# A hybrid decoder trunk on one core: scratch buffers placed by the plan, sums kept in the tiles of x, and a planner that lets two engines wait

## The chip, the cores and the metric

The kernel runs on one core of a Trainium2 chip. The core has a matrix engine (TensorE, PE; its weight loads are the rows PEld), a vector engine (VectorE, DVE), a scalar engine (ScalarE, ACT), GpSimd (POOL), and a queue that issues nearly all transfers (SyncE, SP). Each engine runs its own list of instructions strictly in order, and waits on semaphores for the others. The metric is device time of one execution in microseconds (us). The kernel before took 2038.9 us, the median of three runs (2038.4 to 2039.33).

## The reference

Two layers on an x of 1024 tokens by 1024 channels in float32:

```
for l in range(2):
    h = rmsnorm(x, attn_norm[l]);  proj = h @ w_in[l]
    c_q, c_kv, k_r, g_b, g_c, u_conv, u_pool, q_sw, k_sw, v_sw = split(proj)
    y_a = latent attention(c_q, c_kv, k_r)      # 4 heads, causal, rotary part
    y_b = g_b * conv3(g_c * u_conv)             # short gated convolution
    y_c = pool(u_pool)                          # causal means over 2/4/8/16
    y_d = sliding-window attention(q_sw, k_sw, v_sw)
    mixed = [y / rms(y) for y in (y_a, y_b, y_c, y_d)] * mix_norm[l]
    x = x + mixed @ w_o[l]
    gate, up = split(rmsnorm(x, ffn_norm[l]) @ w_gate_up[l])
    x = x + (silu(gate) * up) @ w_down[l]
return rmsnorm(x, final_norm)
```

The result must be accurate to float32, so each operand of a product is split into a high and a low part (ScalarE casts the high one, VectorE subtracts for the low one), and a product is three matmuls: high by high, high by low, low by high.

## The kernel before

Everything is kept transposed: 128 channels on the partitions, tokens along the row, in two halves of 512. Large tiles live in 47 pairs of slots (`Slots`), each pair 128 x 1024 in four-byte words; small scratch tiles of 128 x 512 come from `tmp`, which has three rings: 2 tiles "te", 3 "tn", 3 "tp". Sums of matmuls go to the eight PSUM banks.

Each layer has a *mixer stage* (about 50 to 430 us and 1050 to 1440 us of the profiled span): the projections, the four mixers, their norms and the output projection. It has many short steps in which TensorE, ScalarE and VectorE hand work to each other. Then come the FFN (to about 800 and 1800 us) and the down-projection. Both use a scheme with seven products in place of eight for 2 x 2 blocks, over the two halves of tokens and pairs of channel blocks, for which sums and differences of the operands are needed: `combine(j)` makes those of x for channel blocks 2j and 2j+1 (its inputs are named a0, b0, a1, b1, the two blocks in the two token halves; its results N1, N2, T3, T4), and `GateUp.sums` those of the weights, on GpSimd.

The lines that the text speaks of: `mm3` (L344) issues nearly all matmuls; `split` (L364 and L367 without a gain, L369 and L370 with one) splits operands; `weights` (L238, L239; L231 where the low part was prepared) splits a weight tile; `mul_to` (L445) multiplies two tiles; `SumSq.rnorm` (L424 to L439) makes the reciprocal of a root mean square; `scores` (L1064 to L1066 the products of queries and keys, L1069 to L1102 the softmax); `mix_values` (L1118, L1130); `combine` (L1229 to L1240, with `minus`, L1219); in the FFN, `GateUp.start`, `n2` (L1358 copies a PSUM bank out), `n1` (L1366), `snap` (L1408), `neg_mul` (L1534), `silu` (L1540 on ScalarE, L1542 the multiplication on GpSimd).

What sets the order of the work is a planner, `Order`, that runs while the program is built. It has a cost for each instruction, walks the program by list scheduling (of what is ready on an engine, the one with the lowest rank starts; ranks come from a pass from the end backwards), tries some thirty random changes near the places where its model has TensorE wait, and imposes the best order on every engine. From its planned end times it also picks the PSUM bank of each PSUM tile (`banks`) and the slot pair of each large tile (`ends`). `scheduled_kernel` does this for two settings (`SLOW`, the costs of VectorE and ScalarE as they are or 3% up) and takes the plan with the best mean over trials with random delays. The rule by which an engine takes its next operation is in `run`:

```
due(e, t)                          # what is ready by t goes into now[e]
k = heapq.heappop(now[e])[1]       # the lowest rank of these starts
```

## Time and profile before

| | |
|---|---|
| time, median of 3 runs | 2038.9 us (2038.4 to 2039.33) |
| profiled execution, first to last instruction (span) | 2037.3 us |
| granted TensorE clock, mean | 0.998 |
| PE busy | 2022.8 us, 99% of the span |
| VectorE busy | 1541.0 us, 76% |
| ScalarE busy | 1020.8 us, 50% |
| GpSimd busy | 565.8 us, 28% |
| HBM traffic | 170 GB/s over the span |

The profile has no other time of that execution than its span; the median of the runs is 1.6 us above it.

How to read its rows: in a row of the timeline stand the start, the duration, the engine, the line, the operation, output and inputs, partitions by elements, the count of instructions merged into the row, and in brackets the idle time before it and what ended it. A matmul's record is longer than the step from one matmul to the next, since matmuls overlap. In a row of a table of stretches stand the stretch, its length, the busy time (with the number of instructions) of PE, PEld, DVE, ACT and POOL, the granted clock as a share, the share of DMA busy and GB/s.

### The profile page before, as it was taken

Reading aid. Unit: us, or ns where it says so; the run is one execution under the profiler, and the core shown is the slowest. Engines: PE = TensorE matmul, PEld = TensorE weight load, DVE = VectorE, ACT = ScalarE, POOL = GpSimd, SP = SyncE. Lnnn points to the kernel's source line nnn. Section 1 sums busy time; section 2 is a strip of 40 time slices with the busy share of each in tenths; the row PEclk is TensorE's granted clock in tenths of the full one; section 3 lists DMA queues with packets and bytes.
Section 4 is the critical chain, followed back from the end, with each engine's and each line's share of the span. In section 5 each row is a group of like instructions: output and inputs, shape, how many; then the busy total and the mean of one; then the engine's idle time right before and its main releaser. Section 6 shows DMA issues by size and latency. Waiting matters only on the chain.

```text
span 2037.3 us, 26734 instructions
## 1 busy us (share of the span) xinstructions
PE 2022.8 (99%) x9418; PEld 1678.6 (82%) x9418; DVE 1541.0 (76%) x2442; ACT 1020.8 (50%) x1778; POOL 565.8 (28%) x428
## 2 busy tenths in 40 slices
PE   9999999999999999999999999999999999999998
PEld 7887888878888888888888878888888888888887
DVE  8779979997667768767646898889976766875555
ACT  7447657753333335555533676677433333354343
POOL 0100000047776782000001000000677777710000
PEclk9999999999999999999999999999999999999999
DMA  6431232434555546998835233242455555487552
GB/s 210 104 64 47 72 102 82 149 124 170 183 182 185 180 169 246 364 349 314 288 113 122 63 93 122 92 144 94 147 192 172 193 175 172 155 308 254 178 186 85
DMA packets 154087, 338.56 MB, mean 166 GB/s; under 512 B 14944, under 2 KB 62048, under 8 KB 153952
## 3 DMA queue, kind: packets, MB, share of 16 engines
q1 hardware_dynamic: 149472, 325.31, 46.3%
q0 software_dynamic: 4480, 11.54, 3.2%
q8 instruction: 74, 1.21, 0.3%
q14 instruction: 61, 0.50, 0.1%
HBM read 241.36 MB, written 105.91 MB: 170 GB/s over the span
## 4 chain that ended last, share of the span: by engine, by line
PE 95%; DVE 2%; DMA 1%; issue 1%; ACT 1%; POOL 0%; SPq 0%; DVEq 0%; POOLq 0%; ACTq 0%
PE ps_mm L344 37%; PE ps_s L344 28%; PE ps_t L344 12%; PE ps_pv L344 8%; PE ps_pv L1130 2%; PE ps_t L1118 1%; PE ps_s L1064 1%; PE ps_s L1066 1%; PE ps_s L1065 1%; PE ps_s L678 1%; PE ps_s L936 1%; PE ps_pv L739 1%; PE ps_t L727 1%; DVE u L367 1%; PE ps_t L424 0%
## 5 line engine op out<-in xcount | busy, mean ns | idle before, releaser
L344 PE MATMUL ps_mm<-u,u 128*128 128x512 f32 (+1 forms) x3378 | 832.4, 390 | 2.2 <-DVE tn L436 0.6
L344 PEld LDWEIGHTS ps_mm<-u,u 128*128 128x128 f32 x3378 | 617.4, 188 | 124.9 <-issue 3.1
L367 DVE TENSOR_TENSOR u<-u,u 128x1024 fp32r<-128x1024 f32 (+3 forms) x429 | 497.0, 1181 | 193.2 <-ACT u L364 131.4
L344 PE MATMUL ps_s<-u,u 128*128 128x512 f32 x2670 | 635.1, 390 | 0.7 <-ACT u L1358 0.5
L364 ACT CAST u<-u 128x1024 fp32r<-128x1024 f32 (+3 forms) x429 | 370.6, 882 | 438.6 <-PE ps_mm L344 62.4
L344 PEld LDWEIGHTS ps_s<-u,u 128*128 128x128 f32 x2670 | 501.5, 188 | 106.2 <-ACT u L1358 1.4
L344 PE MATMUL ps_t<-u,u 128*128 128x512 f32 (+1 forms) x1124 | 256.2, 378 | 0.1
L344 PEld LDWEIGHTS ps_t<-u,u 128*128 128x128 f32 x1124 | 202.7, 188 | 41.2 <-DVE u L1534 2.5
L1542 POOL TENSOR_TENSOR tp<-tp,u 128x512 f32<-128x512 f32 x80 | 126.9, 1586 | 347.8 <-ACT tp L1540 211.3
L344 PE MATMUL ps_pv<-u,u 128*128 128x512 f32 x744 | 177.3, 390 | 0.0
L344 PEld LDWEIGHTS ps_pv<-u,u 128*128 128x128 f32 x744 | 139.7, 188 | 28.9
L318 POOL DMA_DIRECT2D gd<-in_w_gu x24 | 21.2, 885 | 416.3 <-PE ps_t L344 280.9
L1127 POOL MEMSET u<- 128x128 f32 x32 | 6.3, 222 | 426.7 <-PE ps_pv L1130 117.6
L1540 ACT ACTIVATE tp<-tp 128x512 f32<-128x512 f32 x80 | 50.6, 632 | 131.5 <-DVE tp L445 131.4
L364 ACT CAST u<-ps_t 128x512 fp32r<-128x512 f32 (+3 forms) x132 | 64.6, 503 | 55.4 <-PE ps_t L1118 29.1
L367 DVE TENSOR_TENSOR u<-ps_t,u 128x512 fp32r<-128x512 f32 (+3 forms) x132 | 74.8, 581 | 13.9 <-ACT u L364 13.1
L1620 POOL TENSOR_TENSOR u<-u 128x352 f32<-128x352 f32 x64 | 79.3, 1240 | 9.8 <-DMA u<-in_w_dn 9.2
L369 ACT ACTIVATE u<-u,par 128x512 fp32r<-128x512 f32 x99 | 69.5, 717 | 23.3 <-DVE u L445 9.4
L1620 POOL TENSOR_TENSOR u<-u,u 128x352 f32<-128x352 f32 x64 | 76.7, 1199 | 2.6
L370 DVE SCALAR_TENSOR_TENSOR u<-u,par,u 128x512 fp32r<-128x512 f32 x99 | 72.9, 749 | 5.3 <-ACT u L369 5.2
L445 DVE TENSOR_TENSOR tp<-tp,u 128x512 f32<-128x512 f32 x76 | 73.9, 973 | 2.0
L1330 POOL TENSOR_TENSOR u<-u 128x512 f32<-128x512 f32 x38 | 67.4, 1773 | 27.3 <-DVE u L367 27.3
(209 smaller groups left out, 2316.6 us busy)
## 6 DMA issues: line engine op xcount, KB each, us to landing
u<-in_w_gu SPq DMA_DIRECT2D x84, 512.0 KB, 4.0
ad<-u SPq DMA_DIRECT2D x154, 256.0 KB, 2.3
u<-ad SPq DMA_DIRECT2D x70, 512.0 KB, 5.6
u<-in_w_dn SPq DMA_DIRECT2D x64, 352.0 KB, 3.5
qd<-u SPq DMA_DIRECT2D x64, 352.0 KB, 3.1
u<-in_w_in SPq DMA_DIRECT2D x43, 512.0 KB, 5.8
u<-qd SPq DMA_DIRECT2D x32, 512.0 KB, 5.4
u<-in_w_dn SPq DMA_DIRECT2D x24, 512.0 KB, 5.6
```

The lines of the kernel that those rows point to most:

```text
L318: paced(pool.dma_start(d, a, **more))
L344: last_mm = pe.matmul(o, w, r, start=start and k == 0 and i == 0, stop=stop and k == n - 1 and i == 2, skip_group_check=again,)
L364: a = act.copy(hi, f)
L367: dve.tensor_tensor(out=lo, in0=f, in1=rd(hi), op=ALU.subtract)
L369: a = act.activation(hi, f, AF.Copy, scale=gain)
L370: dve.scalar_tensor_tensor(out=lo, in0=f, scalar=gain, in1=rd(hi), op0=ALU.mult, op1=ALU.subtract)
L445: dve.tensor_tensor(out=o, in0=a, in1=b, op=ALU.mult)
L1130: pe.matmul(py[:, c0:], v_of(j, h), R.ap(s)[:, c0:], start=j == 0 and n == 0, stop=j == nj - 1 and n == 1,)
L1330: pool.tensor_tensor(out=q4, in0=q4, in1=F.ap(self.raw[1] + 1), op=ALU.add)
L1540: last_silu = act.activation(g, g, AF.Silu)
L1542: pool.tensor_tensor(out=g, in0=g, in1=r, op=ALU.mult)
L1620: pool.tensor_tensor(out=o, in0=a, in1=b, op=ALU.add)
```

## The change

Five things change.

First, `combine` no longer takes six scratch tiles. It scales b0 and b1 where they are, and writes N1 over a0, T3 over b0 and T4 over a1; N2 alone has a scratch tile.

Second, scratch tiles get their place from the plan, as PSUM banks did. On the first pass the rings have 2, 3 and 2 tiles; afterwards each scratch tile gets one of seven buffers (`N_TMP`). `banks` becomes `places(end, prefix, n)`: it takes the place that came free last before the tile's planned start (or, if none is free, the one that comes free first), among those whose previous tile's last user comes earlier in the program.

Third, the planner may let VectorE and ScalarE wait. When it has picked the operation with the lowest rank r that is ready at time t, it looks at those that will be ready before that operation would be done. If one of these is more urgent by over 4 in rank, and comes so soon that the wait is shorter than what it would otherwise wait, the engine stays idle until then.

Fourth, the constants: the separate float32 tile of ones goes; `ones` is the float32 view of `ones_r`, which is cast from a scratch tile of ones. The 128 columns of the constant from which `e_r` is made are no longer kept; they come to a slot by a DMA of their own, and the slot is freed after the cast.

Fifth, the memory that comes free makes 48 pairs of slots, not 47.

```
-N_U = 47
+N_U = 48
+N_TMP = 7
...
-    cst = cpool.tile([P, CC_N], F32, name="cst")
+    cst = cpool.tile([P, CC_E], F32, name="cst")
...
     def tmp(tag="te"):
-        return tpool.tile([P, HT], F32, name=tag, tag=tag, bufs={"te": 2, "tn": 3, "tp": 3}[tag])
+        if given is None:
+            bufs = {"te": 2, "tn": 3, "tp": 2}[tag]
+            return tpool.tile([P, HT], F32, name="tm", tag=tag, bufs=bufs)
+        return tpool.tile([P, HT], F32, name="tm", tag=f"m{next(tmp_of)}", bufs=1)
...
+    ones_r = cpool.tile([P, P], F32R, name="ones_r")
+    ones = rd(ones_r)
+    dve.memset(start := tmp()[:, :P], 1.0)
+    dve.tensor_copy(ones_r, start)
...
-            loads.append(sp.dma_start(cst, ins["const"]))
+            loads.append(sp.dma_start(cst, ins["const"][:, :CC_E]))
+            spread = F.half()
+            loads.append(sp.dma_start(F.ap(spread)[:, :P], ins["const"][:, CC_E:]))
...
-            dve.tensor_copy(e_r, cst[:, CC_E : CC_E + P])
+            dve.tensor_copy(e_r, F.ap(spread)[:, :P])
+            F.free(spread)
...
-            v0, v1 = tmp("te"), tmp("te")
-            act.activation(v0, b0, AF.Copy, scale=g0)
-            act.activation(v1, b1, AF.Copy, scale=g1)
-            n1, n2, t3, t4 = tmp("tp"), tmp("tp"), tmp("tp"), tmp("tp")
+            act.activation(b0, b0, AF.Copy, scale=g0)
+            act.activation(b1, b1, AF.Copy, scale=g1)
+            n2 = tmp("tp")
             dve.scalar_tensor_tensor(
-                out=n1, in0=a0, scalar=g0, in1=v0, op0=ALU.mult, op1=ALU.subtract
+                out=a0, in0=a0, scalar=g0, in1=b0, op0=ALU.mult, op1=ALU.subtract
             )
-            minus(n2, n1, v1)
+            minus(n2, a0, b1)
...
-            dve.tensor_tensor(out=t3, in0=v1, in1=v0, op=ALU.subtract)
-            hb[T3][j] = half_split(t3)
+            dve.tensor_tensor(out=b0, in0=b1, in1=b0, op=ALU.subtract)
+            hb[T3][j] = half_split(b0)
...
+    PATIENT = ("DVE", "Activation")
+    URGENT, WORTH = 4.0, 1.0
...
-                k = heapq.heappop(now[e])[1]
+                r, k = heapq.heappop(now[e])
+                if e in self.PATIENT:
+                    over = t + cost[k][1]
+                    w = [
+                        x
+                        for x, j in later[e]
+                        if (x - t) * self.WORTH < over - x and rank[j] < r - self.URGENT
+                    ]
+                    if w:
+                        heapq.heappush(now[e], (r, k))
+                        free[e] = min(w)
+                        continue
...
-    def banks(self, end):
+    def places(self, end, prefix, n):
...
-            b = max(range(8), key=lambda b: free[b] if free[b] <= start else -free[b])
+            b = max((b for b in range(n) if last[b] < self.users[m][0]), key=lambda b: free[b] if free[b] <= start else -free[b])
...
-            given = plan.banks(end), plan.ends(end, asked)
+            given = (plan.places(end, "ps_", 8), plan.places(end, "tm_", N_TMP)), plan.ends(end, asked)
```

Since the planner's rule and the buffers change, the order of all engines is made anew. The program has the same instructions on TensorE, ScalarE, VectorE and GpSimd, and one DMA more. In the FFN and down-projection stages TensorE's order is the same row by row; in the mixer stages most of its rows, and those of VectorE and ScalarE, stand elsewhere. The line numbers of the changed program are some four to seven higher. Three places, with the names as the two programs have them (u is a slot pair with its number and the number of the tile in it, tm, te, tn, tp are scratch).

*Place A, ScalarE in layer 1, around the norm of the convolution's group.* L433 to L435 make the norm; the two L369 scale the normed tiles for the output projection; L238 with 128x768 is the cast of a weight tile for that projection; the others belong to the softmax and to `mix_values`. Before:

```order
L433 ACTIVATE tn_2281<-ps_t_2278 128x512
L364 CAST u28_2320<-te_2318 128x512
L434 ACTIVATE tn_2281<-tn_2281 128x512
L435 ACTIVATE tn_2282<-tn_2281 128x512
L1083 ACTIVATE u30_2363,sm2_2364<-ps_s_2366,sm1_2365 128x512
L1086 ACTIVATE u27_2303,sm2_2364<-ps_s_2370,sm1_2365 128x384
L364 CAST u32_2417<-ps_t_2413 128x384
L1100 ACTIVATE u46_2324<-u46_2324,sm2_2344 128x512
L238 CAST u15_2487<-u20_2485 128x768
L364 CAST u33_2425<-ps_t_2422 128x256
L369 ACTIVATE u22_2290<-u12_721,par_75 128x512
L369 ACTIVATE u4_2293<-u8_2072,par_75 128x512
```

and now, from the cast on (L242 is the former L238, L373 the former L369, L437 to L439 the norm):

```order
L242 CAST u10_2486<-u35_2484 128x768
...
L437 ACTIVATE tm_2282<-ps_t_2279 128x512
L438 ACTIVATE tm_2282<-tm_2282 128x512
L439 ACTIVATE tm_2283<-tm_2282 128x512
...
L368 CAST u29_2320<-tm_2318 128x512
L1090 ACTIVATE u30_2324,sm2_2344<-ps_s_2346,sm1_2345 128x512
L373 ACTIVATE u21_2291<-u12_723,par_75 128x512
L1093 ACTIVATE u14_155,sm2_2325<-ps_s_2331,sm1_2326 128x128
L373 ACTIVATE u23_2294<-u36_2074,par_75 128x512
```

The weight cast, which stood two rows ahead of the first scaling, now stands twelve rows ahead of it, before the norm's own three steps.

*Place B, TensorE in layer 1, the first FFN blocks.* ps_s_4163 and ps_s_4280 (now ps_s_4157 and ps_s_4269) are the banks that take the products with N2 and, after `n2` has copied them out, those with T3; ps_mm are the banks of `n1`. Before:

```order
L344 MATMUL ps_mm_4419<-u20_4351,u6_4416 128x512
L344 MATMUL ps_s_4163<-u16_2216,u2_4155 128x512
L344 MATMUL ps_s_4163<-u14_2204,u35_4156 128x512
L344 MATMUL ps_s_4280<-u16_2216,u13_4159 128x512
L344 MATMUL ps_s_4280<-u14_2204,u9_4160 128x512
L344 MATMUL ps_s_4163<-u26_4148,u41_4394 128x512 x2
L344 MATMUL ps_s_4163<-u26_4148,u27_4395 128x512
```

and now:

```order
L348 MATMUL ps_mm_4377<-u27_4138,u1_4373 128x512
L348 MATMUL ps_s_4157<-u47_2205,u20_4149 128x512
L348 MATMUL ps_s_4269<-u47_2205,u31_4153 128x512
L348 MATMUL ps_s_4157<-u15_2217,u20_4149 128x512
L348 MATMUL ps_s_4157<-u47_2205,u0_4150 128x512
L348 MATMUL ps_s_4269<-u15_2217,u31_4153 128x512
L348 MATMUL ps_s_4269<-u47_2205,u8_4154 128x512
L348 MATMUL ps_mm_4377<-u27_4138,u1_4373 128x512
L348 MATMUL ps_mm_4398<-u27_4138,u28_4394 128x512 x2
L348 MATMUL ps_s_4157<-u40_4142,u1_4373 128x512 x2
L348 MATMUL ps_s_4269<-u40_4142,u28_4394 128x512 x2
```

Between the last product with N2 into ps_s_4163 and the first with T3 stood two matmuls; there are five now for each bank. The whole group stands 23 matmuls earlier, ahead of most of the products into the ps_mm banks.

*Place D, TensorE in layer 2, the first scores and a projection of the gated convolution.* ps_mm_10926 and ps_mm_10951 (now ps_mm_10905 and ps_mm_10930) are the two token halves of the projection, ps_s the scores of the first head (L1064 to L1066, now L1071 to L1073). Before:

```order
L344 MATMUL ps_mm_10926<-u2_8900,u24_10829 128x512
L1064 MATMUL ps_s_11005<-u26_10709,u5_10923 128x256
L1065 MATMUL ps_s_11005<-u26_10709,u5_10923 128x256
L1064 MATMUL ps_s_11015<-u26_10709,u5_10923 128x384
L1065 MATMUL ps_s_11015<-u26_10709,u5_10923 128x384
L1066 MATMUL ps_s_11005<-u26_10709,u5_10923 128x256
L1066 MATMUL ps_s_11015<-u26_10709,u5_10923 128x384
L1064 MATMUL ps_s_10995<-u26_10709,u5_10923 128x256
L1065 MATMUL ps_s_10995<-u26_10709,u5_10923 128x256
L1066 MATMUL ps_s_10995<-u26_10709,u5_10923 128x256
L344 MATMUL ps_mm_10951<-u3_8969,u29_10828 128x512 x2
```

and now (the 21 matmuls of the second half that are left out between stand in the same order as before):

```order
L348 MATMUL ps_mm_10905<-u0_8879,u35_10808 128x512
L348 MATMUL ps_mm_10930<-u21_8948,u29_10807 128x512 x2
L348 MATMUL ps_mm_10930<-u21_8948,u35_10808 128x512
...
L348 MATMUL ps_mm_10930<-u46_8889,u35_10808 128x512
L1071 MATMUL ps_s_10984<-u41_10688,u24_10902 128x256
L1072 MATMUL ps_s_10984<-u41_10688,u24_10902 128x256
L1071 MATMUL ps_s_10994<-u41_10688,u24_10902 128x384
L1072 MATMUL ps_s_10994<-u41_10688,u24_10902 128x384
```

The scores stood between the two halves of the projection; the second half, 24 matmuls, now stands ahead of them.

More of the change, by code (lines that the diff above doesn't have):

```diff
@@ L51 @@
 PC_N = 39
-CC_ID, CC_E, CC_TRI, CC_SWA, CC_FIX, CC_INVW = 0, 128, 256, 768, 1792, 1824
+CC_ID, CC_TRI, CC_SWA, CC_FIX, CC_INVW, CC_E = 0, 128, 640, 1664, 1696, 1698
 CC_N = 1826
@@ L145, in trunk_kernel @@
     par = cpool.tile([P, PC_ALL], F32, name="par")
-    cst = cpool.tile([P, CC_N], F32, name="cst")
+    cst = cpool.tile([P, CC_E], F32, name="cst")
     ident = cst[:, CC_ID : CC_ID + P]
-    ones = cpool.tile([P, P], F32, name="ones")
-    dve.memset(ones, 1.0)
-    ones_r = cpool.tile([P, P], F32R, name="ones_r")
-    dve.tensor_copy(ones_r, ones)
     e_r = cpool.tile([P, P], F32R, name="e_r")
@@ L175, in trunk_kernel @@
     }
-    bank_of = iter(given or ())
+    bank_of, tmp_of = map(iter, given or ((), ()))
     def ps(tag):
@@ L1247, in combine @@
             )
-            hb[T4][j] = half_split(t4)
+            hb[T4][j] = half_split(a1)
             for n in range(2):
@@ L2060, in due @@
                 heapq.heappush(now[e], (rank[k], k))
-        for _ in range(self.n):
+        todo = self.n
+        while todo:
             best = None
@@ L2083, in run @@
                 due(e, t)
-                k = heapq.heappop(now[e])[1]
+                r, k = heapq.heappop(now[e])
[10 more added lines that the diff above has]
+                        continue
+            todo -= 1
             seen, taken = cost[k]
@@ L2176, in tiles @@
         return sorted(found, key=lambda m: int(m.rsplit("_", 1)[1]))
-    def banks(self, end):
-        free, given = [0.0] * 8, []
-        for m in self.tiles("ps_"):
+    def places(self, end, prefix, n):
+        free, last, given = [0.0] * n, [-1] * n, []
+        for m in self.tiles(prefix):
             start = min(end[k] - self.cost[k][0] for k in self.users[m])
-            b = max(range(8), key=lambda b: free[b] if free[b] <= start else -free[b])
+            b = max((b for b in range(n) if last[b] < self.users[m][0]), key=lambda b: free[b] if free[b] <= start else -free[b])
             free[b] = max(end[k] for k in self.users[m])
+            last[b] = self.users[m][-1]
             given.append(b)
```

4 lines of the change are left out of this document (2 added, 2 removed).

## The prediction

> **What bounds the kernel now.** I read the page first, then busy time by stage, then the timeline wherever TensorE (PE) stood still. The page says who works and who ends last:
>
> ```profile
> span 2037.3 us, 26734 instructions
> PE 2022.8 (99%) x9418; PEld 1678.6 (82%) x9418; DVE 1541.0 (76%) x2442; ACT 1020.8 (50%) x1778; POOL 565.8 (28%) x428
> PE 95%; DVE 2%; DMA 1%; issue 1%; ACT 1%; POOL 0%; SPq 0%; DVEq 0%; POOLq 0%; ACTq 0%
> ```
>
> PE is busy for 99% of the span and 95% of the chain of waits runs through it. The change removes no matmul (the two programs have the same 9397), so only its pauses can be won. Where they lie, by stage (span, then busy us of PE, PEld, DVE, ACT, POOL):
>
> ```profile
> 50.00:430.00 380.00, 378.26 (x1854) 312.33 (x1853) 331.81 (x736) 237.66 (x514) 17.91 (x29) 1.00 0.30 88
> 430.00:1000.00 570.00, 569.95 (x2513) 471.55 (x2512) 418.34 (x436) 248.19 (x327) 261.13 (x181) 1.00 0.67 235
> 1050.00:1440.00 390.00, 388.33 (x1916) 323.46 (x1915) 326.93 (x736) 245.09 (x528) 21.12 (x32) 1.00 0.36 108
> 1440.00:1985.00 545.00, 544.95 (x2401) 450.46 (x2400) 373.81 (x387) 214.21 (x282) 263.68 (x181) 1.00 0.57 195
> 850.00:900.00 50.00, 50.00 (x222) 41.42 (x222) 31.57 (x36) 24.52 (x32) 0.00 (x0) 1.00 0.95 349
> 150.00:200.00 50.00, 49.98 (x228) 39.06 (x227) 47.95 (x91) 39.72 (x77) 0.00 (x0) 1.00 0.14 45
> 1400.00:1450.00 50.00, 49.71 (x220) 40.82 (x219) 45.62 (x63) 29.26 (x46) 14.40 (x8) 1.00 0.22 72
> ```
>
> The FFN and down-projection stages (rows two and four) have 0.05 us of PE pause each. The mixer stages (rows one and three) have 1.74 and 1.67 us, and there VectorE is nearly as full as PE: the last two rows are the first and the last of eight stretches of 50 us in which it is busy for 45 us or more. The records understate a pause, since a matmul's record is 0.39 us long while the next starts 0.227 us after it (25.16 us for 111 below). So I count from start to start:
>
> ```profile
> 805.10 25.16 PE ps_s L344 x111
> ```
>
> A second measure of the room: the fifth row above, without any pause, has PEld busy for 41.42 / 50 = 0.828; the whole span has 1678.6 / 2037.3 = 0.824. At 0.828 throughout, the span would be 1678.6 / 0.828 = 2027 us: some 10 us is all that can be won. The Trainium skill (Perfetto Trace Analysis, Identifying the Most-Contended Engine) says to judge TensorE by the busy share of LDWEIGHTS and not of matmuls; 82% would by itself promise 18%, or 360 us. The trace does not bear that out, since its fullest stretch stands at 83%.
>
> **The pauses that the new order can touch.** A, layer 1, the norm of the convolution's group (normed values scaled on ACT L369, then split on DVE L370):
>
> ```profile
> 236.75 1.28 DVE L445 TENSOR_TENSOR u<-u,u 128x512 f32<-128x512 f32 x2
> 237.41 0.82 ACT L238 CAST u<-u 128x768 fp32r<-128x768 f32 x1
> 238.20 0.42 PE L1130 MATMUL ps_pv<-u,u 128*128 128x384 f32 x1
> 238.40 1.34 ACT L369 ACTIVATE u<-u,par 128x512 fp32r<-128x512 f32 x2
> 239.18 0.49 PE L344 MATMUL ps_mm<-u,u 128*128 128x512 f32 x1 [0.56 <-ACT u L369]
> 239.97 1.20 PE L344 MATMUL ps_mm<-u,u 128*128 128x512 f32 x4 [0.29 <-DVE u L370]
> ```
>
> ScalarE began a weight cast just as the first normed half was about to be ready. 0.98 us pass from 238.20 to 239.18 where a step of 384 columns needs 0.17 (three quarters of 0.227), then 0.79 where one needs 0.23: 1.37 us lost.
>
> B, layer 1, `combine` and the first FFN blocks:
>
> ```profile
> 421.13 1.53 PE L344 MATMUL ps_mm<-u,u 128*128 128x512 f32 x6
> 422.48 3.41 POOL L1542 TENSOR_TENSOR tp<-tp,u 128x512 f32<-128x512 f32 x1 [13.45 <-ACT tp L1540]
> 423.10 2.82 PE L344 MATMUL ps_mm<-u,u 128*128 128x512 f32 x10 [0.44 <-ACT u L364]
> 425.75 0.62 PE L344 MATMUL ps_s<-u,u 128*128 128x512 f32 x2
> 426.21 0.84 PE L344 MATMUL ps_mm<-u,u 128*128 128x512 f32 x3
> 427.26 1.20 PE L344 MATMUL ps_s<-u,u 128*128 128x512 f32 x4 [0.21 <-DVE u L367]
> 428.67 3.71 PE L344 MATMUL ps_s<-u,u 128*128 128x512 f32 x15 [0.21 <-ACT u L1358]
> ```
>
> From 421.13 to 428.67 are 7.54 us for 6 + 10 + 2 + 3 + 4 = 25 matmuls of 0.227: 1.87 us lost.
>
> C, D and E, all in layer 2 (the norm of the convolution's group, the first scores, the same FFN blocks as in B):
>
> ```profile
> 1195.67 1.76 PE L344 MATMUL ps_mm<-u,u 128*128 128x512 f32 x7
> 1197.89 0.50 PE L424 MATMUL ps_t<-u,ones_r 128*128 128x512 f32 x1 [0.46 <-ACT u L364]
> 1207.61 0.56 PE L1066 MATMUL ps_s<-u,u 128*128 128x256 f32 x2
> 1208.33 0.39 PE L1064 MATMUL ps_s<-u,u 128*128 128x256 f32 x1 [0.16 <-DVE te L445]
> 1208.67 0.28 PE L1066 MATMUL ps_s<-u,u 128*128 128x256 f32 x1
> 1208.85 0.68 DVE L436 SCALAR_TENSOR_TENSOR tn<-ps_t,tn 128x512 f32<-128x512 f32 x1
> 1209.59 0.74 PE L344 MATMUL ps_mm<-u,u 128*128 128x512 f32 x2 [0.64 <-DVE tn L436]
> 1433.75 0.62 PE L344 MATMUL ps_pv<-u,u 128*128 128x512 f32 x2
> 1434.66 1.20 PE L344 MATMUL ps_s<-u,u 128*128 128x512 f32 x4 [0.29 <-ACT u L1358]
> ```
>
> C: 2.22 us less 7 steps (1.59) is 0.63. D: 1.98 us from 1207.61 to 1209.59, less five short steps (four of 0.11, one of 0.17, together some 0.62), is 1.36; its larger half waits for DVE L436 to read a PSUM bank out. E: 0.91 less 0.45 is 0.46. Together 1.37 + 1.87 + 0.63 + 1.36 + 0.46 = 5.7 us.
>
> **The change, part by part.** The rows of both orders stand ahead of this text.
> *Waiting for the more urgent.* A: the 768-wide cast now stands 12 rows ahead of the two scalings, not right in front of them. I take 1.2 of the 1.37 us as won (bounds 0 and 1.37). D: the second token half of a projection for the convolution now follows the first half directly, and in the built program its bank was last read by an L449 (formerly L445) on VectorE that stands 11 rows ahead of the norm's L440 (formerly L436), for which the old one waited; the scores moved some 5 us of matmuls (24 x 0.227) behind it. I take 1.2 of 1.36. C: the norm's matmul stands 4 matmuls later on PE (0.9 us) with its producers on ACT and DVE two rows earlier; I take 0.4 of 0.63, as the chain in front of it is the same.
> *Sums in the tiles of x.* The same two scalings, four sums and four splits per `combine`, of the same sizes: no time of their own is added. What goes is the wait for one of 2 + 3 scratch tiles: in layer 1 the scalings of the second to fourth pair come 10 to 20 ScalarE rows earlier. What comes is that b0 and b1 are overwritten, so their scaling waits for the store to `xr`, the square and the split, and ScalarE's casts for B stand behind it.
>
> ```profile
> ad<-u SPq DMA_DIRECT2D x154, 256.0 KB, 2.3
> ```
>
> For the last pair the scalings stand 11 and 17 ScalarE rows behind the split of the same tile, some 7 us at 0.67 each (A's 1.34 for two), and a store of that size lands in 2.3 (this row): covered. Uncovered it would be 2.3 us in each layer. In B the last sum's split is 8 VectorE rows earlier (8 x some 0.65 = 5.2 us) but its matmul 23 matmuls earlier (5.2 us): nothing won there. The copy L1364 (formerly L1358) now has five other matmuls between the last product of N2 and the next onto the same bank, formerly two: the 0.37 us before 428.67 won. The splits of the next weights are used by short pieces first; in all I take 1.1 of 1.87. E is the same place in layer 2, now with five matmuls between for two: 0.3 of 0.46.
> Together 1.2 + 1.2 + 0.4 + 1.1 + 0.3 = 4.2 us won, with bounds 0 and 5.7.
> *Scratch by plan and the 48th pair.* The planner takes the scratch buffer that came free last before its start, so one buffer is used once and the work runs on six. In the FFN that ties the copy k1 (L1408) to VectorE's product of the previous block:
>
> ```profile
> L1408 ACT COPY tn<-ps_s 128x512 f32<-128x512 f32 x61 | 35.8, 587 | 66.1 <-PE ps_s L344 65.5
> L1542 POOL TENSOR_TENSOR tp<-tp,u x80: 1279/1299/3409, 406.5 to 1818.4; 128x512 f32<-128x512 f32 x80
> ```
>
> PE needs that copy only after twelve matmuls (2.72 us) and the copy takes 0.587: 2.1 us of cover, behind 0.73 DVE occupancy (418.34 / 570). Cost taken: 0; bounds 0 and, without cover, 0.2 us in each of 38 blocks. The pair lets loads start earlier in stages where no PE wait is put down to a load: 0.
> *Constants.* `ones_r` is now what the warm matmuls read, so they start one cast (0.23) later; and e_r comes through a slot by a DMA of its own:
>
> ```profile
> 1.04 0.23 DVE L151 CAST ones_r<-ones 128x128 fp32r<-128x128 f32 x1
> 9.69 0.30 PEld L344 LDWEIGHTS ps_mm<-u,u 128*128 128x128 f32 x2 [0.53 <-DVE u L370]
> 15.30 0.33 SPq L591 DMA_DIRECT2D cst<-in_const  x1
> 180.11 0.73 PE L953 MATMUL ps_t<-u,e_r 128*128 128x512 f32 x2
> ```
>
> At 9.69 PE waits for VectorE anyway and takes the 0.23 in; e_r is first read at 180 us, 160 after its load, which costs SP one more issue of 0.33. Uncovered, 0.6 us in all; taken: 0.
> *New waits.* Nearly every PE row of the mixer stages now stands elsewhere, and an order that fits the planner's costs will miss the chip's at new places. The nearest price is what the old order of the same kind left: 5.7 us. I take a third, 1.9, because the rule that is added works against this kind of loss; bounds 0 and 5.7, and more if VectorE becomes the bound (below).
> Sum: 2037.3 - 4.2 + 1.9 = 2035.0 us of span. The span is the profiled execution's own time as far as it is shown; the runs' median is 1.6 above it, which I carry over: **2036.6 us**.
>
> **The rivals.** *The gain is given back*: as much is lost at new places as won (5.7 is the price of either), 2037.5 to 2040. For it: VectorE at 96% in the mixer stages, so an order can only shift its lateness. Against: A and D were a choice of order and no lack of capacity.
> *All of it comes*: A to E gone and little new: 2038.9 - 5 = 2034 down to 2031, with the smaller pauses. For it: three of the five changed places have the late operation several rows ahead. Against: B hangs on VectorE's total.
> *Slower, by holes in VectorE*: a planned wait becomes a wait in the queue, for the engine runs its list in order. What was put off stands behind an operation that may come late, as B's POOL product did, with 3.41 us against a median of 1.30. In the eight full stretches VectorE has 2 to 5 us left of 50; a hole of 1 us that does not fall into these pushes PE by as much. It decides from 0.8 us per stretch on (8 x 0.8 = 6.5, which is the 2.3 won and the 4.1 that can be told); at 1 us each it is 8 - 2.3 = +5.7 us: 2044.6. The Trainium skill (SBUF — State Buffer, on the shared port pair) has VectorE and GpSimd exclude each other for a whole instruction; by it such a late product is the rule beside long VectorE runs, and 3.41 agrees.
> *It does not do what it says*: the same order where it matters. The FFN's PE order is indeed the same row by row, and nothing can come from there; for the mixers the rows speak against it.
>
> **How the numbers follow.** The forecast has 0.42, the gain given back 0.22, all of it 0.22, slower 0.10, the change without effect (2038.9) 0.04. A measurement of this kernel tells some 0.2%, 4.1 us, from no change. Faster by more than that, below 2034.8, is all of the third case and the edge of the forecast: 0.24. Slower by more, above 2043, is most of the fourth: 0.08. The rest, 0.68, is within. The range goes from 2032.5 (the middle of "all of it") to 2040.5 (just past the gain given back) and leaves out about 0.1 on each side.
>
> **What would show it.** A right: ACT's 768-wide cast lies before the norm's end and PE has no pause over 0.3 us at the first products with the scaled tiles. B and E: no wait for the copy L1364, perhaps one for DVE's split. D: no PE wait for DVE L440. FFN rows: PE pause still 0.05 us. It is wrong if PE's pauses in 50 to 430 and 1050 to 1440 us are over 4 us, if VectorE has waits there on ACT or POOL of over 1 us with PE waiting behind, or if the FFN stages show pauses at the copy L1414.

## The result, and the profile after

| | before | after |
|---|---|---|
| time, median of 5 runs | 2038.9 us (2038.35 to 2039.33) | 2032.24 us (2031.71 to 2032.76) |
| ratio, with its 95% interval | | 0.9968 (0.9958 to 0.9979) |
| span of the profiled execution | 2037.3 us | 2030.0 us |

The kernel is 6.7 us faster, 4.4 more than forecast, and 0.3 us below the range. The page of the kernel after (span; busy time by engine; the chain of waits by engine):

```profile
span 2030.0 us, 26831 instructions
PE 2018.6 (99%) x9418; PEld 1676.7 (83%) x9418; DVE 1531.2 (75%) x2442; ACT 1022.6 (50%) x1778; POOL 567.5 (28%) x428
PE 96%; DVE 0%; DMA 0%; ACT 0%; issue 0%; DVEq 0%; ACTq 0%
```

TensorE does the same work in less time. Its pauses by the table of stretches (span, then busy us of PE, PEld, DVE, ACT, POOL):

```profile
50.00:430.00 380.00, 379.84 (x1867) 315.18 (x1867) 336.14 (x740) 240.04 (x516) 21.39 (x29) 1.00 0.31 90
430.00:1000.00 570.00, 570.00 (x2516) 471.76 (x2515) 409.91 (x436) 247.01 (x324) 263.02 (x181) 1.00 0.67 235
1050.00:1440.00 390.00, 389.40 (x1920) 324.03 (x1919) 334.63 (x737) 245.82 (x526) 24.83 (x34) 1.00 0.36 106
1440.00:1985.00 545.00, 545.00 (x2406) 451.30 (x2405) 366.19 (x392) 215.76 (x288) 255.56 (x177) 1.00 0.57 196
```

The mixer stages (rows one and three) hold 13 and 4 matmuls more than before in the same time; the FFN stages (two and four) hold 3 and 5 more, though they had seemed full. Behind the start, six waits of TensorE are left in the list of waits, each of 0.3 us or less but for the one at the very end (L435). The three longest:

```profile
PE ps_s L435 <- ACT tm L434: 0.5, 1, 0.5
PE ps_mm L348 <- ACT u L368: 0.3, 1, 0.3
PE ps_mm L348 <- DVE u L374: 0.2, 1, 0.2
```

To see where the time went I compare, in both traces, when the n-th of the 9418 matmul records starts. That counts pauses of any length. The matmuls are not all of one size and stand in another order, so each piece ends where both programs have done the same matmuls. (At record 1200, say, the kernel after has done four matmuls of 512 columns more and four of 128 fewer; pieces that met there would be some 0.6 us off.) Time won (-) or lost (+) in each piece, us:

| piece (matmul records) | what lies in it | after | forecast |
|---|---|---|---|
| 0 to 1000 | start, layer 1 up to 212 us | +0.06 | 0, in part "new waits" |
| 1000 to 1250 | place A | -1.44 | -1.2 |
| 1250 to 2014 | rest of the mixer stage | -0.04 | in "new waits" |
| 2014 to 2200 | place B | -2.06 | -1.1 |
| 2200 to 4800 | FFN and down-projection, layer 1 | -0.66 | 0 |
| 4800 to 5630 | places C and D | -2.41 | -1.6 |
| 5630 to 6530 | rest of the mixer stage, layer 2 | +1.30 | in "new waits" |
| 6530 to 6800 | place E | -0.49 | -0.3 |
| 6800 to the last | FFN and down-projection, layer 2 | -1.04 | 0 |
| from the start of the last matmul on | end of the span | -0.56 | 0 |

How far such a piece can be trusted shows in a run below (the weight cast moved) that has TensorE's order of the kernel before: its start, up to record 200, is 1.1 us longer, and each other piece but that of place A lies within 0.3 us of the kernel before.

At B nothing is left: 18 and 12 matmuls follow one another without a wait, and 426.47 - 422.39 = 4.08 us is 18 steps of 0.227.

```profile
422.39 4.24 PE L348 MATMUL ps_mm<-u,u 128*128 128x512 f32 x18
426.47 2.88 PE L348 MATMUL ps_s<-u,u 128*128 128x512 f32 x12
```

Most of the new waits lie in layer 2 (0.47 us is also lost in layer 1, from record 200 to 1000, behind a start that was 0.41 us shorter), and they are short, such as these two (some 0.4 us each from start to start beyond the step):

```profile
1239.19 0.49 PE L1125 MATMUL ps_t<-cst,u 128*128 128x128 f32 x3
1239.90 0.73 PE L348 MATMUL ps_mm<-u,u 128*128 128x512 f32 x2 [0.22 <-DVE u L374]
...
1252.30 0.63 PE L348 MATMUL ps_mm<-u,u 128*128 128x512 f32 x2
1253.12 0.66 PE L1125 MATMUL ps_t<-cst,u 128*128 128x128 f32 x4 [0.19 <-ACT u L1093]
```

### The profile page after: what moved, and what is told of

Its sections match the earlier page's. It is cut to its first block, busy times and chain, and to the rows that moved or that the text cites. A ratio compares the mean times of both kernels' runs of the same rounds, so it can differ in the third digit from the quotient of the medians.

```text
span 2030.0 us, 26831 instructions
## 1 busy us (share of the span) xinstructions
PE 2018.6 (99%) x9418; PEld 1676.7 (83%) x9418; DVE 1531.2 (75%) x2442; ACT 1022.6 (50%) x1778; POOL 567.5 (28%) x428
## 4 chain that ended last, share of the span: by engine, by line
PE 96%; DVE 0%; DMA 0%; ACT 0%; issue 0%; DVEq 0%; ACTq 0%
PE ps_mm L348 37%; PE ps_s L348 30%; PE ps_t L348 12%; PE ps_pv L348 8%; PE ps_pv L1137 2%; PE ps_t L1125 1%; PE ps_s L1071 1%; PE ps_s L1072 1%; PE ps_s L1073 1%; PE ps_s L685 1%; PE ps_s L943 1%; PE ps_pv L746 1%; PE ps_t L734 1%; PE ps_t L428 0%; DMA xp<-u 0%; PE ps_t L431 0%
## 5 line engine op out<-in xcount | busy, mean ns | idle before, releaser
L371 DVE TENSOR_TENSOR u<-u,u 128x1024 fp32r<-128x1024 f32 (+3 forms) x453 | 511.3, 1148 | 194.1 <-ACT u L368 176.5
L368 ACT CAST u<-u 128x1024 fp32r<-128x1024 f32 (+3 forms) x453 | 385.2, 868 | 382.9 <-DMA u<-ad 73.9
L1548 POOL TENSOR_TENSOR tm<-tm,u 128x512 f32<-128x512 f32 x80 | 139.5, 1744 | 341.6 <-ACT tm L1546 337.1
L1546 ACT ACTIVATE tm<-tm 128x512 f32<-128x512 f32 x80 | 50.6, 632 | 135.8 <-DVE tm L449 135.7
L1414 ACT COPY tm<-ps_s 128x512 f32<-128x512 f32 x61 | 35.8, 587 | 101.7 <-PE ps_s L348 101.6
L1626 POOL TENSOR_TENSOR u<-u,u 128x352 f32<-128x352 f32 x64 | 81.4, 1272 | 1.4
L412 ACT ACTIVATE tm<-u 128x512 f32<-128x512 f32 (+1 forms) x91 | 53.9, 600 | 49.2 <-DVE u L1817 41.2
L373 ACT ACTIVATE u<-u,par 128x512 fp32r<-128x512 f32 x99 | 69.4, 715 | 17.8 <-DVE u L1274 7.6
```

Of the source, the lines that this page charges most:

```text
L368: a = act.copy(hi, f)
L371: dve.tensor_tensor(out=lo, in0=f, in1=rd(hi), op=ALU.subtract)
L373: a = act.activation(hi, f, AF.Copy, scale=gain)
L412: act.activation(q, f, AF.Square)
L1414: act.copy(o, p)
L1546: last_silu = act.activation(g, g, AF.Silu)
```

## The experiments

All times are medians of three or more rounds, beside the kernel before on the same chip (2038.4 to 2038.8 us there). "The rule" is the planner's permission to wait. First the whole table; each row is told below.

| pairs of slots | scratch | without the rule, us | with the rule, us |
|---|---|---|---|
| 47 | rings 2, 3, 3, as before | 2038.4 to 2038.9 (before); seed 2: 2039.3 | 2042.4 |
| 46 | seven, by plan | 2053.5 | 2050.5 |
| 47 | seven, by plan | 2038.7; seed 2: 2038.3 | 2036.7; seed 2: 2037.1 |
| 48 | seven, by plan | 2031.2; seed 2: 2031.6 | 2032.2 (after); seed 2: 2031.8 |
| 48 | seven, in rings 2, 3, 2 | 2034.9 | 2032.5 |
| 49 | five, by plan | 2034.6 | 2044.0 |

### Parts alone

**The rule alone.** The kernel before with nothing but the new branch:

```
+                if e in self.PATIENT:   # ("DVE", "Activation")
+                    ...                 # the branch of the change, word for word
```

> The kernel before with the planner's waiting rule alone (scratch rings, combine, 47 pairs as they were). If the waiting rule is what won (theory P: it won the pauses at the norm, in the mixer stage of layer 2, in the FFN stages and in the tail, together about 4.8 us, and the sums in x's tiles won the rest at combine, about 2.4 us): about 2034 us, the FFN stages without a pause, and a pause of 1 to 2 us still at the first FFN blocks. If memory did it (theory M: the 48th pair and the placed scratch): 2039 us, with the FFN pauses there. If it is only a new draw of a random search (theory R): anywhere from 2035 to 2042, with no pattern by stage.

Measured: 2042.41 us, ratio 1.0019 (1.0010 to 1.0029). So the part on which the forecast put most of its gain is slower by 4.0 us when it is alone. By the matmul count 2.7 us of it are lost in layer 1 from record 200 to 1000, 0.6 in the piece of place A, and 1.5 and 1.2 in layer 2, in the rest of the mixer stage and at E. The sign is that of the slower rival, but its mechanism, more holes in VectorE, does not show: VectorE is busy for 333.5 and 327.2 us of the two mixer stages, where it was 331.8 and 326.9. The longest hole that fits is in place B, where VectorE (first two rows) stands idle 1.18 us for a GpSimd product, a split follows, and TensorE (last two rows) waits for that split:

```profile
428.40 0.69 DVE L445 TENSOR_TENSOR u<-ps_s,tp 128x512 f32<-128x512 f32 x1 [1.18 <-POOL tp L1542]
429.01 0.68 DVE L367 TENSOR_TENSOR u<-tp,u 128x512 fp32r<-128x512 f32 x1
...
427.89 0.86 PE L344 MATMUL ps_mm<-u,u 128*128 128x512 f32 x3
429.75 0.96 PE L344 MATMUL ps_s<-u,u 128*128 128x512 f32 x3 [1.00 <-DVE u L367]
```

The kernel before has that hole too, in the same place and without the rule, and with the rule B as a whole is 0.66 us shorter:

```profile
425.92 0.69 DVE L445 TENSOR_TENSOR u<-ps_s,tp 128x512 f32<-128x512 f32 x1 [1.19 <-POOL tp L1542]
```

So why the rule alone is slower stays open.

**All but the rule.** The kernel after with the rule off:

```
-    PATIENT = ("DVE", "Activation")
+    PATIENT = ()
```

> The changed kernel without the waiting rule; all else changed. Theory P: 2037 us, FFN pauses of some 1.7 us in all back, combine without its pause. Theory M: 2032 to 2033 us. Theory R: anywhere from 2031 to 2039.

Measured: 2031.2 us, ratio 0.9963 (0.9948 to 0.9978). The gain is there without the rule. Together with the first run this ends theory P.

**The sums in the tiles of x alone.** The kernel before with the new `combine`, nothing else:

> The kernel before with combine's sums in the tiles of x alone. Theory P: 2036.5 us, the pauses at the first FFN blocks (1.87 and 0.46 us) gone, those in the FFN as before. Theory M: 2036 to 2039, since it too frees scratch. Theory R: anywhere from 2035 to 2042.

Measured: 2036.86 us, 0.9991 (0.9982 to 1.0000): 1.6 us won, at the edge of what these runs can tell. By the matmul count, place B wins 1.93 and E 0.54 us. B wins 1.91 to 2.06 us in each of the sixteen kernels that have these sums, and 0.66 or less in the four that have not (before, its second seed, the rule alone, and the next). So the sums in the tiles of x end the pauses of B. That they do so by the scratch tiles that `combine` no longer takes is the likeliest reason; no run gave the old `combine` more scratch.

**The weight cast at place A moved.** The order of the kernel before, with that one ScalarE cast behind the two scalings that stood after it:

```
+                acts.insert(n + 3, acts.pop(n))   # n: the cast of 128x768, L238
```

> The kernel before in its own order, with one ScalarE instruction moved: the 768-wide weight cast at place A now stands behind the two scalings, not in front of them. If A was a choice of order: the pause of 1.37 us at 238 us is down to 0.3 or less and the time about 2037.6 us (1.3 less). If VectorE's fullness only shifts the lateness: the same 2038.9 us, with the pause at a later place before 430 us.

Measured: 2039.05 us, 1.0002 (0.9993 to 1.0011). ScalarE's rows there, and TensorE's first product (lines are one higher; this execution runs 1.1 us later from the 200th matmul on, long ahead of the moved cast):

```profile
237.87 0.72 ACT L1101 ACTIVATE u<-u,sm 128x512 f32<-128x512 f32 x1
239.13 0.37 ACT L365 CAST u<-ps_t 128x256 fp32r<-128x256 f32 x1 [0.53 <-PE ps_t L1119]
239.40 1.33 ACT L370 ACTIVATE u<-u,par 128x512 fp32r<-128x512 f32 x2
240.63 0.82 ACT L239 CAST u<-u 128x768 fp32r<-128x768 f32 x1
...
240.17 0.50 PE L345 MATMUL ps_mm<-u,u 128*128 128x512 f32 x1 [0.47 <-ACT u L370]
```

The cast is behind the scalings, yet these begin only 0.1 us earlier. Where the cast stood, ScalarE now idles 0.53 us: the 128x256 cast next in its list waits for TensorE's transposes (L1119), and the scalings queue behind that. The pauses at A go from 1.37 to 1.28 us. The weight cast had filled a hole; with it moved, the small cast holds the scalings. In the kernel after, both scalings are ahead of it in the list.

### How far a new draw goes

Two runs change only the seed of the planner's search.

```
-        draw = random.Random(1)
+        draw = random.Random(2)
```

> The changed kernel whole; only the seed of the planner's random search is another one. The two first results to be explained: the waiting rule alone was slower by 4.0 us, and the change without that rule was 1.0 us faster than with it, so theory P (the waits won the time) is out. Left are M: the memory edits (48th pair, scratch placed by plan, sums in the tiles of x) give the planner fewer stalls to work around, so most of the 6.7 us stay whatever the seed: 2031 to 2034.5 us. R: 6.7 us are one lucky draw of the search, and another seed gives another: 2035 to 2041 us is as likely as 2030 to 2035.

> The kernel before; only the seed of the planner's random search is another one. It gives the spread that a new draw makes by itself. M: 2037 to 2041 us, above every kernel that has the memory edits. R: it comes down to where the changed kernel is, 2031 to 2035 us, or rises by as much, to 2042 us or more.

Measured: after 2031.82 us, 0.9966 (0.9953 to 0.9980); before 2039.30 us, 1.0002 (0.9993 to 1.0012). A second draw of the search moves either by 0.4 to 0.7 us. Theory R falls, as far as two draws of each can tell: 6.7 us is ten times what a draw moved.

### The 48th pair, and the placed scratch

The kernel after with one of them taken back:

```
-N_U = 48
+N_U = 47
```

> The changed kernel whole, but with 47 pairs of slots instead of 48. M with the 48th pair as the part that wins: the gain goes back but for the 1.6 us of the sums in the tiles of x, to 2036 to 2039 us. M with the placed scratch as the part: 2032 to 2034 us. R: nothing to be said, 2031 to 2041 us.

```
-        if given is None:
-            ...
-        return tpool.tile([P, HT], F32, name="tm", tag=f"m{next(tmp_of)}", bufs=1)
+        bufs = {"te": 2, "tn": 3, "tp": 2}[tag]
+        return tpool.tile([P, HT], F32, name="tm", tag=tag, bufs=bufs)
```

> The changed kernel whole, but its seven scratch buffers are taken in turn, in rings of 2, 3 and 2 by kind, as before, instead of placed by the plan. M with the placed scratch as the part that wins: back to 2036 to 2039 us. M with the 48th pair as the part: 2032 to 2034 us. R: nothing to be said, 2031 to 2041 us.

Measured: 47 pairs 2036.74 us, 0.9992 (0.9983 to 1.0002); rings 2032.52 us, 0.9969 (0.9957 to 0.9982). The 48th pair is worth 4.5 us, the placed scratch 0.3. With 47 pairs TensorE waits at the norm in layer 2 again (C and D: 1.06 us lost, where the kernel after wins 2.41):

```profile
PE ps_mm L348 <- DVE u L371: 1.3, 1, 1.3
PE ps_mm L348 <- DVE u L1004: 1.1, 2, 0.9
PE ps_t L428 <- DVE tm L440: 1.0, 1, 1.0
```

VectorE waits for no slot there. The first three rows are its own, and from 1189 to 1201.75 us it never pauses for more than 0.05 us. TensorE (last two rows) waits for a VectorE that works without a pause, in another order than in the kernel after:

```profile
1198.54 0.67 DVE L371 TENSOR_TENSOR u<-ps_s,u 64x512 fp32r<-64x512 f32 x1
1199.13 0.68 DVE L443 SCALAR_TENSOR_TENSOR u<-tm 128x512 f32<-128x512 f32 x1
1199.86 0.69 DVE L371 TENSOR_TENSOR u<-ps_s,u 64x512 fp32r<-64x512 f32 x1
...
1198.68 0.74 PE L428 MATMUL ps_t<-u,ones_r 128*128 128x512 f32 x2 [1.00 <-DVE tm L440]
1200.70 1.62 PE L348 MATMUL ps_mm<-u,u 128*128 128x512 f32 x6 [1.28 <-DVE u L371]
```

The same steps without the rule, a second seed there, and PSUM banks given as before (424 of 658 PSUM tiles then lie elsewhere):

> The changed kernel without its waiting rule, and with 47 pairs of slots instead of 48. With the rule, 47 pairs cost 4.5 us (2036.7 against 2032.2 us), most of it at the norm of layer 2's mixer. M (the 48th pair wins, whatever the rule): 2035 to 2037 us. If the rule and the pair only win together or spoil each other: 2031 to 2033 us. For the FFN stages: if the short pauses at the products into ps_t come back (0.75 and 1.0 us over the two stages), the pair is what ended them where there is no rule.

> The changed kernel without its waiting rule and with the scratch in rings of 2, 3 and 2 instead of placed by plan: what is left of the change is the 48th pair, the smaller constants, the sums in the tiles of x, and the rule on PSUM banks. If these are all that wins: 2031 to 2033 us. If the placed scratch stands in for the rule where the rule is gone: 2034 to 2037 us, with the short pauses of the FFN stages back.

> The changed kernel without its waiting rule, with another seed of the planner's search; with the rule two seeds gave 2032.2 and 2031.8 us. If the rule costs a microsecond in the changed kernel: 2030.5 to 2031.5 us again. If 2031.2 us was one draw: 2031.5 to 2033 us.

> The changed kernel without its waiting rule, and with PSUM banks given as before, without the new condition that a bank's last tile must come earlier in the program than the next; the scratch keeps the condition. 424 of 658 PSUM tiles then lie in another bank. If that condition is what lengthened the time between VectorE's last read of a bank and TensorE's next write in the FFN stages: their short pauses come back, 1.7 us, 2033 us. If not: 2031 to 2032 us.

Measured: 47 pairs 2038.72 us, 1.0001 (0.9992 to 1.0011); rings 2034.93 us, 0.9982 (0.9973 to 0.9991); second seed 2031.59 us, 0.9967 (0.9954 to 0.9980); old banks 2030.73 us, 0.9962 (0.9948 to 0.9976). Without the rule, too, the pair decides: 7.5 us, and all of the gain is gone at 47. One part after the other, from the kernel before: the sums in the tiles of x win 1.6 us; seven scratch buffers by plan in place of eight in rings, with the other constants, lose 1.9 (2036.86 to 2038.72); the pair that they pay for wins 7.5; the rule loses 1.0. The rings cost 3.7 us there, of which 1.93 is one pause at 402 us:

```profile
PE ps_s L346 <- ACT u L366: 1.8, 1, 1.8
```

The new condition on PSUM banks is worth nothing that shows.

### What a pair of slots does

Two questions stayed: was 47 pairs a poor draw, and does the time follow the number of slots? (Edits as above: `N_U` of 46, 47 with seed 2, and 49. The last is paid for by scratch, `N_TMP` of 5 and rings 1, 2, 2 in the first pass.)

> The changed kernel without its waiting rule, with 46 pairs of slots. If the number of slots sets the time (theory M, now the 48th pair): slower than at 47 (2038.7 us), 2039 to 2048 us. If 2038.7 us at 47 was a poor draw (theory R): anywhere between 2031 and 2040 us.

> The changed kernel with 47 pairs of slots and another seed of the planner's search; the first seed gave 2036.7 us, with three pauses of 1.18, 1.46 and 1.11 us of TensorE behind the norm of layer 2's mixer. M: 2035 to 2039 us. R: 2031 to 2034.5 us, without these pauses.

> The changed kernel without its waiting rule, with 47 pairs and another seed; the first seed gave 2038.7 us. M: 2036 to 2040 us. R: 2031 to 2035 us.

> The changed kernel without its waiting rule, with 49 pairs of slots, paid for by two of the seven scratch buffers. If slots still bind at 48: 2028 to 2030.5 us. If 48 was the last that counts, or five scratch buffers are too few: 2031 to 2036 us.

Measured: 46 pairs 2053.54 us, 1.0074 (1.0059 to 1.0089); 47 again 2037.05 us, 0.9991 (0.9982 to 1.0001), with the rule, and 2038.27 us, 0.9999 (0.9989 to 1.0008), without; 49 pairs and five scratch buffers 2034.64 us, 0.9983 (0.9973 to 0.9993). 47 pairs was no poor draw, and the second pair counts for less than the first: without the rule 15 us from 46 to 47, 7 from 47 to 48. At 49 two things changed, and the missing scratch can hide what the pair brings; that is not told apart.

How a slot becomes time is plainest at 46 pairs. First VectorE's list, then TensorE's:

```profile
535.98 1.07 DVE L449 TENSOR_TENSOR tm<-tm,u 128x512 f32<-128x512 f32 x1
542.69 0.69 DVE L1540 SCALAR_TENSOR_TENSOR u<-ps_pv,tm 128x512 f32<-128x512 f32 x1 [5.64 <-DMA qd<-u]
...
538.96 1.52 PE L348 MATMUL ps_s<-u,u 128*128 128x512 f32 x6
543.44 1.43 PE L348 MATMUL ps_t<-u,u 128*128 128x512 f32 x5 [2.96 <-DVE u L1540]
```

`neg_mul` (L1540) reads a PSUM bank and writes a slot. The slot's last content is still being stored (`qd<-u`), so VectorE idles 5.64 us; the bank stays taken, and TensorE idles 2.96 us. No load is involved.

The kernel before has the same chain in small, with TensorE in place of the store. VectorE's split (L367) writes its low part to a slot that a matmul is still reading, and `neg_mul` (L1534) queues behind it. VectorE, then TensorE:

```profile
1641.84 2.12 DVE L367 TENSOR_TENSOR u<-u,u 128x1024 fp32r<-128x1024 f32 x1 [1.02 <-PE ps_s L344]
1643.87 0.68 DVE L1534 SCALAR_TENSOR_TENSOR u<-ps_s,tp 128x512 f32<-128x512 f32 x1
...
1639.75 4.92 PE L344 MATMUL ps_s<-u,u 128*128 128x512 f32 x21
1644.61 1.67 PE L344 MATMUL ps_t<-u,u 128*128 128x512 f32 x6
```

L1534 ends at 1644.55, the product into its bank starts at 1644.61. Twenty-one steps from 1639.75 would have put it at 1644.52: 0.09 us lost there, and some 0.1 more at the next step, both hidden inside the 0.39 us records, so that no row of TensorE's matmuls shows a wait. The same block in the kernel after:

```profile
1634.59 1.97 DVE L371 TENSOR_TENSOR u<-u,u 128x1024 fp32r<-128x1024 f32 x1
1636.49 0.68 DVE L1540 SCALAR_TENSOR_TENSOR u<-ps_s,tm 128x512 f32<-128x512 f32 x1
...
1633.74 4.92 PE L348 MATMUL ps_s<-u,u 128*128 128x512 f32 x21
1638.50 1.75 PE L348 MATMUL ps_t<-u,u 128*128 128x512 f32 x7
```

The split did not wait; the bank is free at 1637.17, 1.33 us ahead of its use, and the 21 steps take 4.76 us.

How much VectorE waits for slots in the FFN and down-projection of layer 1 stands in the groups of its instructions from 430 to 1000 us, behind the second bar (idle us ahead of the 135 splits, and what ended it). A matmul writes no slot, so a split of operands that lie in slots and that waits for TensorE or for a store (`ad<-u`) waits for the slot that it is to write. Before; 47 pairs without the rule; 48 pairs without the rule; after:

```profile
L367 DVE TENSOR_TENSOR u<-u,u 128x1024 fp32r<-128x1024 f32 x135 | 190.1, 1425 | 71.3 <-ACT u L364 49.4 <-PE ps_s L344 9.8 <-DMA ad<-u 8.7
L371 DVE TENSOR_TENSOR u<-u,u 128x1024 fp32r<-128x1024 f32 x135 | 188.3, 1408 | 72.8 <-ACT u L368 42.4 <-PE ps_s L348 12.5 <-DMA ad<-u 8.2
L371 DVE TENSOR_TENSOR u<-u,u 128x1024 fp32r<-128x1024 f32 x135 | 174.3, 1299 | 53.6 <-ACT u L368 51.3 <-DMA phin<-u 0.9 <-PE ps_pv L348 0.4
L371 DVE TENSOR_TENSOR u<-u,u 128x1024 fp32r<-128x1024 f32 x135 | 188.0, 1401 | 73.4 <-ACT u L368 71.5 <-POOL u L1626 1.0
```

Slots cost VectorE 9.8 + 8.7 us there before, 12.5 + 8.2 with the pair taken back and the rule off, and about 1 and nothing in the two kernels with 48 pairs. In layer 2 the same rows (1440 to 1985 us) give 25.6, 27.1, 3.3 and 11.8 us: fewer waits for slots with 48 pairs, but in the kernel after not none. The idle time as a whole is no smaller after than before (73.4 and 71.3 us): VectorE now idles for ScalarE's casts of the same operands. What costs TensorE time in the blocks of 46 pairs and of before is a wait with `neg_mul` behind it; the other waits were not followed.

By the matmul count, the FFN's short pauses are gone with 48 pairs in every run, rule or not (0.6 us won or more in each FFN but for one of 0.44), while without the rule they stay with 47 (0.02 and 0.04 us lost in layer 1, 0.26 and 0.56 in layer 2, two seeds). The 15 us from 47 to 46 pairs lie here: 7.9 and 7.3 us in the two FFN stages.

But the rule can end these pauses as well: with it, 47 pairs win 0.75 us in layer 1 and 0.98 or 1.08 in layer 2, as much as 48. So in the kernel after, which has the rule, the FFN gains nothing from the pair. There the pair's worth lies at C and D: 3.5 of the 4.2 us between the two profiles; with the second seed 4.8, more than the 4.2 between those two. For the mixer stages the pair's worth is measured, but it was not followed to single slots; at C and D VectorE, as shown, waits for none. How the pair changes the order there stays open.

### The rule at other numbers of slots

> The changed kernel with its waiting rule, with 46 pairs of slots; without the rule 46 pairs took 2053.5 us, 15 us more than 47, most of it in the FFN stages (two pauses of some 2.5 to 3 us in each), where VectorE waits up to 5.6 us for a store to leave the slot that it is to write. If the rule helps where slots are short, as at 47 pairs (2036.7 against 2038.7): 2040 to 2050 us. If what it did there was one draw: 2050 to 2057 us.

> The changed kernel with its waiting rule, with 49 pairs of slots, paid for by two of the seven scratch buffers; without the rule this took 2034.6 us, against 2031.2 at 48 pairs and seven buffers. If the rule makes up for missing buffers, as it did where the scratch lay in rings (2032.5 against 2034.9): 2030 to 2033 us. If not: 2034 to 2037 us.

Measured: 46 pairs 2050.48 us, 1.0056 (1.0041 to 1.0071); 49 pairs and five buffers 2044.02 us, 1.0027 (1.0017 to 1.0038), where the same without the rule is 9.4 us faster. Over the eight pairs of runs that differ by the rule alone, it changes the time by +4.0 (kernel before), -3.1 (46), -2.0 and -1.2 (47, two seeds), +1.0 and +0.2 (48, two seeds), -2.4 (48, rings) and +9.4 (49). No condition that I tried predicts its sign; that stays open. The 9.4 us lie in no single place: between the two profiles (9.0 us) 1.0 are lost in the mixer stage of layer 1, 1.4 in its FFN, 3.6 and 3.2 in those of layer 2.

The versions without the rule at 48 pairs (2031.2, 2031.6, 2030.7) stand 0.2 to 1.5 us below those with it (2032.2, 2031.8). Their intervals overlap, so none of them is shown to beat the kernel after.

## Why the prediction was wrong

**The bound: right, as an estimate.** TensorE's pauses were all there was to win, and the fastest version won 7.8 us of the 10. But 83% is not the fullest share of weight loads: from 50 to 100 us, where 265 matmuls fit and not 222, it is 42.44 of 50 us, 85%. Nor is VectorE at 96% in the mixer stages: that is the fullest 50 us, and over the two stages it is 331.81 of 380 and 326.93 of 390 us, 87 and 84%.

**"The pair lets loads start earlier in stages where no PE wait is put down to a load: 0"** is the step that failed. It priced the pair at nothing; it measures 4.5 and 5.2 us with the rule and 7.5 and 6.7 without. That is the whole of the missed 4.4 us: with 47 pairs the rest of the change takes 2036.7 and 2037.1 us, where 2036.6 was forecast (by some luck, since the terms below miss on both sides). The step looked only at the reading side of a slot (TensorE waiting for a load). A slot also has a writing side: VectorE waiting for a slot that a matmul or a store still holds. That is shown as a cost at 46 pairs and in the FFN without the rule, and its 9.8 and 8.7 us in the row above stood in the profile of before. It is not shown at C and D, where most of the pair's worth lies in the kernel after; by what path the pair wins there is not known.

**"FFN stages ... nothing can come from there": wrong, by 1.7 us.** TensorE's order was the same, but its pauses of 0.05 us were read from busy time, which the prediction itself said understates a pause. Counted from start to start they held 1.7 us. With 47 pairs and the rule they go too, so the order of VectorE and ScalarE counted where TensorE's order was the same.

**New waits, +1.9: nearly the right size, for a wrong reason.** The pieces of the mixer stages that hold none of A to E sum to 0.06 - 0.04 + 1.30 = +1.3 us. The rule was to hold them down, and at 48 pairs it makes them: behind record 200 these pieces lose 1.7 and 2.1 us with it (two seeds); without it they lose 0.0 and win 0.6.

**A to E: 6.4 us won (1.44 + 2.06 + 2.41 + 0.49), where 4.2 of 5.7 was taken.** It is more than 5.7 because the pieces hold other pauses too. B was undersized (1.1 for 2.06): the sums in the tiles of x take all of it. At A the size was near (1.2 for 1.44) and the reason wrong: the cast "right in front" of the scalings was not what held them (moved away, it wins 0.09 us). A, C and D were put down to the rule. Without it at 48 pairs A wins 1.3 and C with D 1.5 us; with it at 47 pairs, A wins 0.8 and C with D lose 1.1.

**Scratch by plan 0 and constants 0: right in this kernel.** Placed scratch is worth 0.3 us here, though 3.7 without the rule. The first matmul starts 0.26 us later, the 0.23 that was named; the 200th is 0.41 us earlier, which is less than a start of one order can differ (1.1).

**The end of the span, -0.56: not in the sum.** From the start of the last matmul on it took 9.44 us before and 8.88 after. No run tells why.

Sum of the span as it came: -6.40 + 1.32 - 1.70 - 0.56 = -7.34 us, against -2.3. Of the rivals, "all of it comes" had the time (2031 to 2034) and A to E; that little would be new was wrong, and that the order alone would win them, without the pair. "Slower, by holes in VectorE" has the sign of what the rule does alone (2042.4, where 2044.6 was priced), but VectorE's busy time in the mixer stages is no smaller there, so its mechanism is not shown. It did not come about in the whole change.

## What to carry to other kernels

Price a buffer also by who waits to write it, and not only by who waits for its load: in the waits of the engine that fills it, sum the rows that are released by the buffer's readers and by stores. Even that can miss most of it, as at C and D here; a run with one buffer fewer is the surest price. Where everything is planned at build time, an edit that gives the planner room can be worth more than one that makes it cleverer, and a cleverer rule must be tried at several settings, since its sign can change from one to the next. When a pause stands behind an operation, ask what the next one in that engine's list would wait for if the first were gone; and count pauses from start to start in every stage, also in one that looks full, between points at which both programs have done the same work.

## What the runs showed of the hardware that was not expected

VectorE's 135 splits in the rows above are the same instruction on the same sizes, and yet took 1425, 1408, 1299 and 1401 ns in the mean in these four kernels. What shortens them in the third was not tried.

One order does not start alike in each execution: with the same lists up to place A as in the kernel before, the profiled execution with the moved cast had its 200th matmul 1.1 us later. A comparison of single profiles is good to about a microsecond unless it is made piece by piece.
